# Queries and index queries of a sparse-attention block: features on the partitions, stacked per head by way of DRAM in place of PE transposes

## The chip, the cores and the metric

The kernel runs on one core of one Trainium2 chip. Its five engines run side by side, each with its own instruction stream in order: TensorE (PE, matmuls; its weight loads are shown as PEld), VectorE (DVE), ScalarE (ACT), GpSimd (POOL) and SyncE (SP, which here only issues DMAs). They wait for each other by semaphores. Sixteen DMA engines move data between DRAM and the on-chip memory; SP, ACT and POOL each issue to a queue of their own. PE writes its results to eight banks of accumulator memory, and ACT or DVE carry them from there.

The metric is the device time of one execution in microseconds (us), as the median over runs. Before the change it is 763.98 us (three runs, 763.91 to 766.41).

## The reference, cut to what matters

Two layers run over 528 tokens (16 meta tokens ahead of 512) of 1024 features. Every layer projects the normed input into queries (8 heads of 64), one key and one value head, index queries (8 heads of 64), one index key, gates and pooling inputs. Each layer chooses, for every query, the 128 keys with the best index score among those it may see, and attends to these.

```python
q, k, v, gate_a, u_b, gate_b, q_idx, k_idx, w_idx, merge = jnp.split(proj, ...)
q = apply_rope(rms_norm(q.reshape(B, T, N_HEADS_A, HEAD_DIM), qn_g), cos_h, sin_h)
k = apply_rope(rms_norm(k, kn_g), cos, sin)
q_idx = apply_rope(q_idx.reshape(B, T, N_IDX_HEADS, IDX_DIM), cos_h, sin_h)
k_idx = apply_rope(k_idx, cos, sin)
attn = indexer_sparse_attention(q, k, v, q_idx, k_idx, w_idx, k_top)
...
def apply_rope(x, cos, sin):
    half = x.shape[-1] // 2
    rot = jnp.concatenate([-x[..., half:], x[..., :half]], axis=-1)
    return x * cos + rot * sin
```

`apply_rope` is where the two halves of a head, features 0 to 31 and 32 to 63, are mixed: the first half becomes a cos - b sin, the second b cos + a sin.

## The kernel before

**Numbers in two parts.** Products that need more precision than one pass gives are made from a high part (a value rounded to the fast fp32r format) and a low part (what the rounding left). The normed input lies in `hhi` and `hlo`, with features on the partitions and tokens in the free dimension; every weight chunk has a high tile and a low tile. A product is three sums: high by high, low by high, high by low. With 8 blocks of 128 input features that makes 24 matmuls, called a group here.

**Weights.** They come in chunks of 256 output columns (`chunks`, lines 112 to 128), two chunks ahead of their use, by SP into the tiles `raw` (`w_fetch`). `w_prep_enqueue` queues the splitting into high and low: as ACT cast and DVE subtraction (`high`, `low`), or, for chunks in `by_dma`, as a negated ACT copy, an accumulating DMA from POOL's queue (line 202) and a second ACT copy. In each layer chunk 0 and chunk 2 hold the index queries of heads 0 to 3 and 4 to 7, chunk 1 the keys, values and index weights (used unsplit), 3 and 4 and 8 and 9 gates, 5 and 6 the pooling inputs, 7 and 10 the attention queries of heads 0 to 3 and 4 to 7.

**Order.** PE's and DVE's instructions run in the order in which the program writes them; a scheduler orders the other engines and the DMA queues by readiness. Each product group ends with `group_done`, which counts groups, runs what `later(fn, n)` has put n groups off, takes one step of weight splitting, and calls `half_done`. That one, also called in the middle of a group, takes `rate` / 2 steps on average from the queue `fill`, whose entries are generators: `index_steps` (the index scores, lines 627 to 640) and later the attention. Steps of the top-k search (`sel`) are taken when an estimate says that DVE has time. So PE meets the first index step of a tile at a fixed place in its own stream and waits there if the tile isn't complete. `drain` empties `fill` before the pooling inputs.

**A query tile.** `tok_group` (line 481) makes a [128 tokens x 256 features] tile, four heads, with the tokens as stationary operand: 24 matmuls with 256 columns moving. `q_post` (line 585) takes it on: two DVE products with cos and sin tables (the second with the halves swapped) and their sum on POOL; for attention queries also a square on ACT and a sum per head on DVE for the norm (`RQ`, applied later as a scale in the softmax). Groups later follow `second` (ACT casts the high part), `third` (DVE subtracts the low part) and `trans`: four PE transposes, one per head, of [128 tokens x (64 high, 64 low)], and an ACT copy of their bank. The result for each head is a [128 x 128] operand with 64 rows of high parts above 64 of low parts and tokens in the free dimension: `qi` for the index scores, `qq` for the attention, the stationary operands of products with the stacked keys `KI` and `KK`.

**Stages of a layer** (lines 1041 to 1169). A trio of key groups; then index groups for token tiles 1 and 2, key groups for tiles 3 and 4, index groups for tiles 3 and 4 (chunk 0), four index groups from chunk 2; the gate products of chunks 3 and 4; the pooling inputs; `queries(0)` (chunk 7), gates, `queries(1)` (chunk 10); then the attention as fill beside the branch products. In layer 0 `queries` has a fifth tile, the 16 meta tokens, whose normed queries go to `qm`. `index_steps` of a tile enters `fill` FI = 6 groups after its own group; `rate` is 3 in this stage (`R_IDX`) and until the attention. `tables` lets POOL build cos and sin tables times the norm gains, four times in all.

**Tiles.** Temporary tiles share places by tag: six of tag L (544 columns; `r` of the index steps and the attention's rows among them), four of tag P (the stacked parts ahead of their transposes), six of tag tt, eight of tag B (`qi`, `qq` and others).

Of the kernel before, what the change touches and what calls it, by code (L numbers as in the profile page):

```python
# [17 lines left out]
T = 528  # L18
# [11 lines left out]
PB = 4  # L30
R_ATT = (1.95, 1.7)
# [9 lines left out]
R_IDX = 3  # L41
UF = 2
QI = 3
# [45 lines left out]
def tile_block(ctx: ExitStack, tc: tile.TileContext, x, meta, w_in, pool_w, w_a, w_b, w_out, rows, hgain, c_tab, out):  # L89
# [10 lines left out]
    def f(ap):  # L100
        return ap.bitcast(F32)
# [11 lines left out]
    mixed, by_dma, plain = set(), set(), set()  # L113
    for l in range(2):
        wi = w_rows(w_in[l], 0, w_in.shape[2])

        chunks.append([(wi[:, :, 2176:2432], 0)])
# [6 lines left out]
        by_dma |= set(range(len(chunks) - 10, len(chunks)))  # L124
# [38 lines left out]
    def w_prep_enqueue(casts_first=False, after=None):  # L163
# [14 lines left out]
        def split(which):  # L178
            t = w_tile().rearrange("p (k e) -> p k e", e=cols)
            parts[which].extend(t[:, k] for k in range(kt // 2))  # L180
            return t

        his = {}

        def high(s):
            his[s] = split(0)
            act.copy(his[s], raws[c][s])

        def low(s):
            dve.tensor_sub(split(1), raws[c][s], f(his[s]))  # L190
# [193 lines left out]
    gains = one.tile([128, 2, 2, 64], F32, name="gains")  # L384
# [7 lines left out]
    dma(gains, bass.AP(tensor=hgain.tensor, offset=hgain.offset, ap=[[0, 128], [128, 2], [64, 2], [1, 64]]))  # L392
# [27 lines left out]
    Cg = one.tile([128, 5, 64], F32, name="Cg")  # L420
    Sg = one.tile([128, 5, 64], F32, name="Sg")
    BV = one.tile([128, 4, 2, 64], F32, name="BV")
    RQ = one.tile([128, 4, NH], F32, name="RQ")
    NR = one.tile([128, 4, NH], F32, name="NR")
# [4 lines left out]
    def sheet(n, name):  # L429
        if n > HB:  # L430
            return tmp.tile([128, 544], F32, tag="L", name=name, bufs=LB)
        return tmp.tile([128, HB], F32, tag="tt", name=name, bufs=6)

    def tables(l, keys):
        if keys:
            gk = tmp.tile([128, 64], F32, tag="gk", name="gk", bufs=1)
            gp.tensor_scalar(gk, gains[:, 1, l], -0.125, None, op0=OP.mult)
        g = gk if keys else gains[:, 0, l]

        def bc(g):  # L440
            return g[:, None, :].to_broadcast([128, 5, 64])

        def sw(g):
            return g.rearrange("p (a d) -> p a d", a=2)[:, None, ::-1, :].to_broadcast([128, 5, 2, 32])

        s4 = stab.rearrange("p t (a d) -> p t a d", a=2)
        gp.tensor_tensor(Cg, ctab, bc(g), op=OP.mult)
        gp.tensor_tensor(Sg.rearrange("p t (a d) -> p t a d", a=2), s4, sw(g), op=OP.mult)
# [32 lines left out]
    def tok_group(t, w):  # L481
        e = 256
        s, m = TOK[t]
        ps = bank("d")
        for h in H:
            for k in range(KT):
# [883 lines left out]
```

## Time and profile before

| | |
|---|---|
| median of three runs | 763.98 us |
| the profiled execution | 764.77 us |
| its span on the core | 763.0 us |
| instructions in the span | 15629 |
| bytes moved by DMA | 96.94 MB, 127 GB/s |

The page of the profile and its views are of that one execution. A line of the timeline has the start, the duration, the engine, the line in the program (nearly all PE and DVE instructions carry the line of a helper, L61), the operation, the written tile, the tiles that were read, shapes and count. For a matmul "128*16" is the size of the stationary operand and "128x256" the moving one. Durations of neighbouring matmuls overlap, so costs on PE are taken from starts, not from durations. A plain fp32 matmul leaves two records. In the list of groups the last numbers are the busy time in all, the mean in ns, and the engine's idle time ahead of the group with what ended it. In a view of windows each row has the window, its length, then busy time and count of instructions for PE, PEld, DVE, ACT and POOL, the granted clock, the share of the DMA engines and GB/s. A DMA's row has its size and the median time from issue to landing. In the page's line of DMA shares each digit is a fortieth of the span, in tenths.

### The profile page before, as it was taken

Reading aid. Unit: us, or ns where it says so; the run is one execution under the profiler, and the core shown is the slowest. Engines: PE = TensorE matmul, PEld = TensorE weight load, DVE = VectorE, ACT = ScalarE, POOL = GpSimd, SP = SyncE. Lnnn points to the kernel's source line nnn. Section 1 sums busy time; section 2 is a strip of 40 time slices with the busy share of each in tenths; the row PEclk is TensorE's granted clock in tenths of the full one; section 3 lists DMA queues with packets and bytes.
Section 4 is the critical chain, followed back from the end, with each engine's and each line's share of the span. In section 5 each row is a group of like instructions: output and inputs, shape, how many; then the busy total and the mean of one; then the engine's idle time right before and its main releaser. Section 6 shows DMA issues by size and latency. Waiting matters only on the chain.

```text
span 763.0 us, 15629 instructions
## 1 busy us (share of the span) xinstructions
PE 746.0 (98%) x5911; PEld 712.7 (93%) x5911; DVE 555.8 (73%) x1412; ACT 471.4 (62%) x1044; POOL 214.2 (28%) x282
## 2 busy tenths in 40 slices
PE   6999999999999999999999999999999999999998
PEld 5899999999999999999998989988889899999998
DVE  4866887888888776894447668877899888678531
ACT  5668844638788796543245796455577788864320
POOL 2551174334011010063346410761411111005200
PEclk9999999999999999999999999999999999999999
DMA  7567685676031112553422677678811221146411
GB/s 257 179 157 194 151 198 138 142 195 165 2 107 60 56 58 82 168 170 112 140 85 83 166 172 169 172 152 204 204 49 56 85 83 56 57 123 213 138 44 42
DMA packets 73547, 96.94 MB, mean 127 GB/s; under 512 B 3664, under 2 KB 58736, under 8 KB 73472
## 3 DMA queue, kind: packets, MB, share of 16 engines
q1 hardware_dynamic: 67488, 74.83, 30.8%
q0 software_dynamic: 5760, 20.97, 15.1%
q8 instruction: 46, 0.75, 0.4%
q14 instruction: 29, 0.24, 0.1%
q10 hardware_dynamic: 224, 0.15, 0.1%
HBM read 66.41 MB, written 8.55 MB: 98 GB/s over the span
## 4 chain that ended last, share of the span: by engine, by line
PE 79%; DVE 11%; ACT 7%; issue 1%; DMA 1%; POOL 0%; ACTq 0%; DVEq 0%; POOLq 0%
PE d L61 66%; PE a L61 10%; PE v L61 4%; DVE w L61 3%; ACT lt L713 2%; ACT w L233 1%; ACT lt L724 1%; DVE t L61 1%; DVE raw L61 1%; DVE nf L61 1%; DMA par<-in_rows_dram 1%; ACT pt L740 1%; DVE lt L61 1%; DVE c L61 1%; DVE alo L61 1%
## 5 line engine op out<-in xcount | busy, mean ns | idle before, releaser
L61 PE MATMUL d<-hhi,w 128*128 128x256 f32 (+3 forms) x1408 | 287.8, 296 | 0.3 <-DVE c L61 0.2
L61 PEld LDWEIGHTS d<-hhi,w 128*128 128x128 f32 x1408 | 225.9, 188 | 6.1 <-DVE c L61 0.7
L61 PE MATMUL d<-hlo,w 128*128 128x256 f32 (+3 forms) x704 | 193.6, 294 | 0.6 <-DVE hlo L61 0.6
L61 PEld LDWEIGHTS d<-hlo,w 128*128 128x128 f32 x704 | 132.5, 188 | 3.3 <-DVE hlo L61 0.8
L61 PE MATMUL d<-w,hhi 128*128 128x256 f32 (+1 forms) x800 | 124.9, 286 | 0.7 <-DVE w L61 0.5
L61 PEld LDWEIGHTS d<-w,hhi 128*128 128x128 f32 (+1 forms) x800 | 107.3, 185 | 3.8 <-issue 1.2
L61 DVE TENSOR_TENSOR w<-raw,w 128x512 fp32r<-128x512 f32 (+1 forms) x128 | 107.8, 852 | 2.4 <-ACT w L233 2.3
L61 PE MATMUL d<-hsum,w 128*128 128x264 f32 (+1 forms) x576 | 77.1, 286 | 0.1
L725 POOL TENSOR_SCALAR pm<-lt,rs 128x16 f32<-128x16 f32 x48 | 27.3, 583 | 173.5 <-DVE rs L61 166.6
L61 PE MATMUL d<-w,hlo 128*128 128x256 f32 (+1 forms) x400 | 74.5, 281 | 0.0
L61 PEld LDWEIGHTS d<-hsum,w 128*128 128x128 f32 x576 | 71.8, 188 | 1.1 <-ACT lt L724 0.3
L202 POOL DMA_DIRECT2D w<-raw x40 | 36.8, 935 | 104.7 <-ACT w L201 82.7
L233 ACT CAST w<-raw 128x512 fp32r<-128x512 f32 x96 | 56.8, 623 | 3.6 <-DVE raw L61 3.5
L61 PEld LDWEIGHTS d<-w,hlo 128*128 128x128 f32 (+1 forms) x400 | 58.5, 184 | 0.4
L1233 POOL TENSOR_TENSOR hlo<-ta,hhi 128x256 fp32r<-128x256 f32 (+1 forms) x28 | 28.2, 1021 | 96.6 <-PE d L61 84.1
L61 DVE MATCH_REPLACE8 sc<-m,sc 128x400 f32<-128x400 f32 (+2 forms) x100 | 54.3, 548 | 0.0
L61 DVE MAX8 m<-sc 128x8 f32<-128x400 f32 (+2 forms) x100 | 52.7, 556 | 0.8
L713 ACT ACTIVATE lt<-lt,mn,NR 128x144 f32<-128x144 f32 (+3 forms) x64 | 42.3, 665 | 16.5 <-DVE mn L61 16.3
L61 PE MATMUL d<-mhi,w 128*128 128x272 f32 (+2 forms) x192 | 47.6, 328 | 0.0
L201 ACT ACTIVATE w<-raw 128x1024 fp32r<-128x1024 f32 x40 | 41.3, 1057 | 10.2 <-PE d L61 10.2
L61 DVE SCALAR_TENSOR_TENSOR sc<-r,wsg,sc 128x144 f32<-128x144 f32 (+3 forms) x56 | 32.4, 581 | 16.6 <-ACT r L637 14.1
L602 POOL TENSOR_TENSOR t<-t,t 128x256 f32<-128x256 f32 (+1 forms) x34 | 31.1, 916 | 39.4 <-DVE t L61 39.4
(198 smaller groups left out, 1392.1 us busy)
## 6 DMA issues: line engine op xcount, KB each, us to landing
raw<-in_w_in_dram SPq DMA_DIRECT2D x72, 512.0 KB, 3.6
w<-raw POOLq DMA_DIRECT2D x40, 512.0 KB, 5.7
raw<-in_w_out_dram SPq DMA_DIRECT2D x16, 512.0 KB, 3.4
kept<-res SPq DMA_DIRECT2D x16, 264.0 KB, 2.8
res<-kept SPq DMA_DIRECT2D x16, 264.0 KB, 6.1
raw<-in_w_branch_b_dram SPq DMA_DIRECT2D x8, 512.0 KB, 4.2
raw<-in_w_branch_a_dram SPq DMA_DIRECT2D x8, 512.0 KB, 3.7
xt<-in_x_dram SPq DMA_DIRECT2D x4, 512.0 KB, 6.3
```

The costliest lines, as they stand in the source:

```text
L61: return fn(*a, **k)
L201: act.activation(t, raws[c][s], AF.Copy, scale=-1.0)
L202: gp.dma_start(t, raws[c][s], accum_op=OP.add)
L233: act.copy(t[:, 0], blk[src[n]])
L602: gp.tensor_tensor(t1[:m, :256], t1[:m, :256], t2[:m, :256], op=OP.add)
L713: act.activation(L[hh][:, :n], L[hh][:, :n], AF.Exp, scale=NR[:, i, h:h + 1], bias=mn[:, hh:hh + 1], accum_out=sm[:, hh:hh + 1])
L724: act.activation(L[hh][:, 16:n], L[hh][:, 16:n], AF.Copy, scale=rs[:, hh:hh + 1])
L725: (gp if j < 3 else dve).tensor_scalar(pms[i][:, 2 * j + hh, :], L[hh][:, 0:16], rs[:, hh:hh + 1], None, op0=OP.mult)
L740: act.copy(pt[:, :2 * len(bs)], tp[:, :256 * len(bs)].rearrange("p (a c) -> p a c", c=128))
L1233: pool_end = gp.tensor_sub(hlo[:, j, a:a + n], d, f(hhi[:, j, a:a + n]))
```

## The change

A query pair replaces two query tiles. `query_pair` makes, for half of the tokens, four heads at once: two groups (`dense` with `turn`) with the weights as stationary operand and the tokens moving. The weight chunks 0, 2, 7 and 10 are `turned`: split with their columns reordered, so that the first group gives the first rotary halves of the four heads (4 x 32 features on the partitions) and the second group the second halves. All four are split by ACT and DVE; 7 and 10 no longer by accumulating DMA. `first` multiplies a group by cos and sin (`CS`, both tables turned once at the start by 20 matmuls) and, for attention queries, by the gain per feature (`gq`) in one DVE instruction with two output halves; POOL combines the halves of both groups. `second` casts the high part, `third` subtracts the low part and writes both, head by head, into a DRAM tile `via` whose rows are in the stacked order (eight DMAs from SP); `fourth` reads the stacked tiles back (two DMAs from POOL, three with the meta tokens). There are no transposes of queries any more. The norms' sums of squares over features become two small PE products per pair (`norms`). Meta tokens ride in the first half of layer 0's queries; their scale is applied in `meta_attn`. Index steps enter `fill` five groups after the pair's own two; `rate` becomes 4 (`R_GATE`) behind the index stage. `tables` is gone; `kv_post` multiplies by the key gain itself. Tag tt has five places instead of six.

```diff
+        turned |= {len(chunks) + i for i in (0, 2, 7, 10)}
...
-        by_dma |= set(range(len(chunks) - 10, len(chunks)))
+        by_dma |= set(range(len(chunks) - 10, len(chunks))) - turned
...
+            if c in turned:
+                parts[which].extend(t.rearrange("p (a k e) -> p k a e", a=2, k=4)[:, k] for k in range(4))
+                return t.rearrange("p (a h d) -> p a h d", a=2, d=32)
...
+            return raws[c][s].rearrange("p k (h a d) -> p a (k h) d", a=2, d=32) if c in turned else raws[c][s]
...
+    for h in range(4):
+        dma(gq[32 * h:32 * h + 32].rearrange("p l a -> p (l a)"),
+            bass.AP(tensor=hgain.tensor, offset=hgain.offset, ap=[[1, 32], [32, 4]]))
...
+    def turned_tables():
...
+        for c, tab in enumerate((ctab, stab)):
+            for ts_ in ((0, 1, 2), (3, 4)):
+                tp = bank("a")
...
+                    for o in (0, 64):
+                        pe.matmul(tp[o:o + 64, s - a:s - a + m], tab[:m, t], ident[:m, :m], start=True, stop=True)
...
-    def tok_group(t, w):
...
-    def q_post(t, ps, normed, dst, g=0):
...
+    def query_pair(l, g, hf, w, normed, dst, between=None):
+        a, n = (HB, T - HB) if hf else (0, HB) if normed and l == 0 else (16, HB - 16)
+        M, sq = [None, None], [None, None]
+        via = dram.tile([128, 4, n], F32, name=f"via{l}{g}{hf}{int(normed)}")
+        rows_of = via.rearrange("(s a d) h t -> s h d a t", s=2, a=2)
+
+        def first(b, ps):
+            m = M[b] = tmp.tile([128, 544], F32, tag="L", name="turned", bufs=LB)[:, :2 * n].rearrange(
+                "p (c n) -> p c n", c=2)
+            p2 = ps[:, None, :n].to_broadcast([128, 2, n])
+            if normed:
+                dve.scalar_tensor_tensor(m, p2, gq[:, l, b:b + 1], CS[:, :, a:a + n], op0=OP.mult, op1=OP.mult)
+                sq[b] = tmp.tile([128, HB], F32, tag="tt", name="sq", bufs=TB)[:, :n]
+                act.activation(sq[b], ps[:, :n], AF.Square, scale=HD ** -0.5)
+            else:
+                dve.tensor_tensor(m, p2, CS[:, :, a:a + n], op=OP.mult)
+            if b:
+                gp.tensor_tensor(M[0][:, 0], M[0][:, 0], m[:, 1], op=OP.subtract)
+                gp.tensor_tensor(M[0][:, 1], M[0][:, 1], m[:, 0], op=OP.add)
...
+        def second():
+            t = part("qhi")[:, :2 * n].rearrange("p (c n) -> p c n", c=2)
+            parts.append(t)
+            act.copy(t, M[0])
+            if normed:
+                dve.tensor_add(sq[0], sq[0], sq[1])
+
+        def third():
+            t = part("qlo")[:, :2 * n].rearrange("p (c n) -> p c n", c=2)
+            dve.tensor_sub(t, M[0], f(parts[0]))
+            parts.append(t)
+            for s, p in enumerate(parts):
+                for h in range(4):
+                    dma(rows_of[s, h], f(p[32 * h:32 * h + 32]))
+            if normed:
+                norms()
+
+        def norms():
+            sp = bank("a")
+            for x_ in range(2):
+                o = TOK[1 + 2 * hf + x_][0] - a
+                pe.matmul(sp[:, 4 * x_:4 * x_ + 4], sq[0][:, o:o + 128], heads4, start=True, stop=True)
...
+        def fourth():
+            todo = [(dst[x_], TOK[1 + 2 * hf + x_][0] - a, 128) for x_ in range(2)]
+            if a == 0:
+                todo.append((qm[:, 4 * g:4 * g + 4], 0, 16))
+            for d, o, m in todo:
+                gp.dma_start(d, via[:, :, o:o + m])
+
+        for b in range(2):
+            ps = dense(w, b, a, n, turn=True)
+            later(lambda b=b, ps=ps: first(b, ps), 1)
+            if b:
+                for k, fn in enumerate((second, third, fourth)):
+                    later(fn, 2 + k)
+            if between:
+                between(b)
+            group_done()
...
+        def index_queries(hf, g, w, between=None):
+            qi = [tmp.tile([128, 4, 128], F32R, tag="B", name="qi", bufs=8) for _ in range(2)]
+            query_pair(l, g, hf, w, False, qi, between)
+            for x_ in range(2):
+                later(lambda x_=x_: fill.append(index_steps(2 * hf + x_, g, qi[x_])), FI - 1)
...
+        index_queries(0, 0, w, second_half)
+        for t in (3, 4):
+            ps = plain_group(t, raws[kv])
+            later(lambda t=t, ps=ps: kv_post(l, t, ps), 1)
             group_done()
...
+        index_queries(1, 0, w)
...
+        for hf in range(2):
+            index_queries(hf, 1, w, lambda b, hf=hf: keep(2 * hf + b))
...
+        rate[0] = R_GATE
```

More of the change, by code (lines that the diff above doesn't have):

```diff
@@ L30 @@
 PB = 4
+TB = 5
 R_ATT = (1.95, 1.7)
@@ L41 @@
 R_IDX = 3
+R_GATE = 4
 UF = 2
-QI = 3
 LEAD = 5
```

216 lines of the change are left out of this document (90 added, 126 removed).

## The prediction

> **What bounds the kernel now.** I read the engines' busy shares first, then the chain of work that ended last, then what the TensorE (PE) waited for.
>
> ```profile
> PE 746.0 (98%) x5911; PEld 712.7 (93%) x5911; DVE 555.8 (73%) x1412; ACT 471.4 (62%) x1044; POOL 214.2 (28%) x282
> ...
> DMA  7567685676031112553422677678811221146411
> ...
> PE 79%; DVE 11%; ACT 7%; issue 1%; DMA 1%; POOL 0%; ACTq 0%; DVEq 0%; POOLq 0%
> ```
>
> PE is busy for 746.0 of 763.0 us, and 79% of the chain is its work. Of PE's own waits the edit touches one, of transposes for their operand:
>
> ```profile
> PE a L61 <- DVE qs L61: 0.4, 1, 0.4
> ```
>
> So the change is worth the PE work that it removes, less what it adds, less the waits that it puts in PE's in-order stream. I call the two token (or feature) groups of an index pair A1, A2 (first half of the tokens, heads 0 to 3), A3, A4 (second half), B1 to B4 (heads 4 to 7), the late key groups K3, K4, and the gate groups behind them C1 to C8. PE runs A1 A2 K3 K4 A3 A4 B1..B4 C1..C8.
>
> **PE work removed.** One index group with the transposes around it, and an output group without any, from the chain of waits:
>
> ```profile
> 56.69 0.45 PE L61 MATMUL a<-identr,qs 128*128 128x128 f32 x4
> 56.98 1.18 PE L61 MATMUL d<-w,hhi 128*128 128x256 f32 x8
> ...
> 59.89 0.46 PE L61 MATMUL a<-identr,qs 128*128 128x128 f32 x4
> ```
> ```profile
> 60.79 1.51 PE d L61 x12
> ...
> 65.27 1.43 PE d L61 x12
> ...
> 710.93 2.84 PE d L61 x24
> ```
>
> From transposes to transposes it is 59.89 - 56.69 = 3.20 us, against 2.84 us for 24 bare matmuls: 0.36 us for four transposes and the restart. There are 128 of them:
>
> ```profile
> L61 PE MATMUL a<-identr,qs 128*128 128x128 f32 x128 | 14.7, 238 | 0.4 <-DVE qs L61 0.4
> ...
> L61 PE MATMUL d<-w,hhi 128*16 128x256 f32 x32 | 4.6, 285 | 0.0
> ```
>
> 128 / 4 x 0.36 = **11.5 us**. The new groups have 24 matmuls of 256 columns as the old ones do, only with weights as the stationary operand, so they cost the same 2.84 us. The 16 meta tokens, though, had a group of their own in each query chunk of layer 0 (the second row above counts 32 of its 48 matmuls), at the full 256 columns:
>
> ```profile
> 119.87 1.10 PE L61 MATMUL d<-w,hlo 128*16 128x256 f32 x8
> 120.80 1.10 PE L61 MATMUL d<-w,hhi 128*16 128x256 f32 x8
> 121.75 1.05 PE L61 MATMUL a<-us,pw 128*128 128x272 f32 x4
> ...
> 132.13 0.48 PE L61 MATMUL a<-identr,qs 16*128 16x16 f32 x4
> 132.54 1.21 PE L61 MATMUL d<-w,hhi 128*128 128x256 f32 x8
> ```
>
> Sixteen take 121.75 - 119.87 = 1.88 us, so 24 take 2.82, and the small transposes 0.41: twice 3.2 = **6.5 us**. In exchange 96 matmuls have 272 columns, which is 1.51 against 1.43 us per 12 in the chain above, so +0.6 us.
>
> **PE work added.** The squares are now summed over partitions by matmuls with one full fp32 tile as weights. The row statistics of the output stage are that form:
>
> ```profile
> 398.36 0.28 PE L61 MATMUL a<-ones,sqs 128*128 128x1 f32 x2
> ...
> 399.24 2.88 PE L61 MATMUL v<-raw,nf 128*16 128x200 f32 x16
> ```
>
> Four such matmuls lie between 398.36 and 399.24 (two records each), 0.22 us each; 18 of them (two in each of 8 query pairs, two for the meta tokens) and eight restarts of 0.07 are 4.5 us. The turned cos and sin tables need 20 half-array fp32 matmuls of 128 columns, once. The attention's value products are that form:
>
> ```profile
> 205.30 2.11 PE v L61 x24
> ...
> 230.76 2.99 PE v L61 x40
> ```
>
> Both have the same four meta products; the 16 further records (8 matmuls) cost 0.88 us, 0.11 each, so 2.2 us. PE work in all: -11.5 - 6.5 + 0.6 + 4.5 + 2.2 = **-10.7 us**.
>
> **The new trip through DRAM.** Per pair SP issues eight 64 KB writes, four for the high part and four for the low part; POOL then issues two 256 KB reads (three with the meta tokens) that wait for all eight. No such trip is in the trace; these are its nearest rows:
>
> ```profile
> raw<-in_w_in_dram SPq DMA_DIRECT2D x72, 512.0 KB, 3.6
> ...
> kept<-res SPq DMA_DIRECT2D x16, 264.0 KB, 2.8
> ...
> out_dram<-ot SPq DMA_DIRECT2D x16, 128.0 KB, 1.7
> far<-nf SPq DMA_DIRECT2D x4, 264.0 KB, 4.6
> ...
> hsheet<-far SPq DMA_DIRECT2D x3, 264.0 KB, 3.7
> ```
> ```profile
> L202 POOL DMA_DIRECT2D w<-raw x40: 850/876/1288, 49.0 to 546.4; - x40
> ...
> DMA to landing us min/median/max: 4.5/5.7/8.5
> ```
> ```profile
> L1316 SPq DMA_DIRECT2D out_dram<-ot x16: 332/332/356, 714.5 to 760.2; - x16
> ```
>
> Four issues at 0.33 us, after the last low part, are 1.4 us. A write lands between 1.7 us (quiet) and 4.6 us (busy stage); I take 2.8, the row with the same burst of writes to DRAM. The read lands between 3.7 and 8.5 us; I take 5.0, half the bytes of the POOL row but 512 short runs. The trip is 1.4 + 2.8 + 5.0 = 9.2 us behind the low part; bounds 6.8 and 14.5.
>
> When is the low part there? Its place in VectorE's order (DVE) is that of the old one, `third`:
>
> ```profile
> 38.43 0.42 DVE L61 TENSOR_TENSOR qs<-t,qs 128x256 fp32r<-128x256 f32 x1
> ...
> 51.20 0.42 DVE L61 TENSOR_TENSOR qs<-t,qs 128x256 fp32r<-128x256 f32 x1
> ```
> ```profile
> 34.55 2.95 PE L61 MATMUL d<-raw,nf 128*128 128x200 f32 x16 [0.63 <-DVE t L61]
> 37.43 1.27 PE L61 MATMUL a<-identr,ks 16*128 16x16 f32 x12
> 38.54 1.18 PE L61 MATMUL d<-w,hhi 128*128 128x256 f32 x8
> ...
> 52.99 0.46 PE L61 MATMUL a<-identr,ks 128*128 128x128 f32 x4
> ```
>
> For the first tile it ran 1.0 us after K4's end at 37.43; for the third, due behind B2, 1.8 us before B2's end at 52.99. The new one is twice as wide (0.7 us), so it ends 1.7 us after its group in pair A1-A2 and 1.1 us before it in the others. PE asks for the result three groups on, when the first index step comes out of the fill queue. Pair A1-A2: twelve key transposes (38.54 - 37.43 = 1.1), three groups (8.5), four key transposes (0.36): 10.0 us, against 1.7 + 9.2 = 10.9, so PE waits **0.9 us in each layer**. Pair A3-A4: B3, B4, C1 and some five index steps, about 10.5 us, against 8.1, no wait. For B1-B2 and B3-B4 the gates and up to eight steps make it 13 and 11.5 us, no wait. The attention queries are asked for later still: the third unit of the attention, first to read heads 4 to 7, is seven fill steps behind the last pair at 1.95 a group.
>
> The Trainium skill's page "DMA: Bandwidth & Descriptors" (Anatomy of one DMA) puts a transfer at 2.0 us plus its bytes at 436 GB/s, about 2.2 us for a write and 2.6 for a read here as an estimate; by that no pair waits and the sum would be 1.8 us lower. Its section Rules for kernel authors speaks against the change (under 64 KB a transfer is mostly overhead), and the row of 4.6 us for 264 KB shows that this fit is a quiet chip's.
>
> **Everything else.** Chunks 7 and 10 of each layer are now split by ACT and DVE instead of an accumulating DMA: 8 more wide DVE subtractions, 8 fewer ACT passes.
>
> ```profile
> L61 DVE TENSOR_TENSOR w<-raw,w 128x1024 fp32r<-128x1024 f32 x32 | 42.9, 1357 | 0.1
> ...
> L201 ACT ACTIVATE w<-raw 128x1024 fp32r<-128x1024 f32 x40 | 41.3, 1057 | 10.2 <-PE d L61 10.2
> ...
> L61 DVE TENSOR_TENSOR qs<-t,qs 128x256 fp32r<-128x256 f32 x32 | 13.3, 416 | 0.0
> ```
>
> That is +10.9 us on DVE and -8.5 on ACT. Against it two old tiles cost DVE six 256-wide operations (2.5 us; the attention queries also two reductions and two small adds), a new pair three 512-wide ones at about 0.7 (the attention queries also one add). Over 16 pairs that is about -9 us, so DVE keeps its load, and ACT loses its 32 evictions. While top-k still runs there is little room: PE 19.9 and DVE 19.0 of 20 us here.
>
> ```profile
> 560.00:580.00 20.00, 19.92 (x131) 17.29 (x130) 19.02 (x57) 14.61 (x41) 1.34 (x5) 1.00 0.06 17
> ```
>
> I charge 1.0 us (bounds 0 and the refund below). At B1, PE already waits for DVE's low halves of chunk 2; when it comes 0.7 us sooner it waits that much more, but that is the same place as the 0.9 us above, so the two overlap. The four tiny gain loads at the start hold SP back by four issues, 1.3 to 1.6 us; the second half of the kv weights behind them is not read before the middle of the first key group, so nothing is charged (at worst 1.5). The rotary tables that POOL no longer builds were off PE's path.
>
> **Sum.** 764.77 (profiled run, 763.0 span and 1.8 around it) - 10.7 + 2 x 0.9 + 1.0 = 756.9; that run lies 0.8 above the median of 763.98, so **756.1 us**.
>
> **Rivals.** (1) *Loaded queues, slower than before.* One mechanism: write and read together take 4.6 + 8.5 = 13.1 us instead of 7.8, because the stage's DMA queues are full (the page's DMA line has 5 to 8 tenths in the first ten slices). With x us more, a layer's waits are 0.9 + x, then x - 2.4, x - 3.4 and x - 4.9 where positive. At x = 5.3 that is 6.2 + 2.9 + 1.9 + 0.4 = 11.4, twice 22.8: 764.77 - 10.7 + 22.8 + 1.0 - 0.8 = 777. It ends above the old time once a layer loses 4.9 us, at x = 3.2. For it: POOL's 512 runs of 512 bytes have no row. Against: raw loads of 1 KB runs land in 3.6 us in the same stage. (2) *The refund.* PE's saving behind the index stage (16 tiles at 0.36, the 6.5, less 5.1) is 7.2 us; if DVE sets the pace of top-k and softmax, all of it comes back as a burst before the attention: 763.3, no change. For it: the last row above; against: PE lost only 0.1 us in that window. (3) *Buffers.* The products take places of the six L tiles that the index steps rotate through (about 2.2 beside the steps' 3.5); should the steps wait for a place, 1.5 us in each of eight index pairs gives 768. PE's four small banks cover most of that.
>
> **Chances.** Forecast 0.56, refund 0.14, loaded queues 0.24, buffers 0.06. No change means within 0.5%, about what a measurement of this kernel can tell: 760.2 to 767.8. Faster 0.57, no change 0.18, slower 0.25. The forecast's own range is 752 (no wait, nothing lost on DVE, and 1 us for the terms) to 760; the range of 8 in 10 reaches to 772, where x is 4.6.
>
> **What would show it.** Right: the rows of transposes with qs and of the 128*16 groups are gone, each index pair's first KI product follows its group with under 1 us idle, and the read lands in about 5 us. Wrong: PE idle in front of KI products at B1 and C1 released by the DMA that fills qi (rival 1), by ACT's r (rival 3), or DVE full from the queries to the attention with PE idle there (rival 2).

## The result, and the profile after

| | time, us (median) | against the kernel before |
|---|---|---|
| before | 764.3 (763.9 to 766.4, 4 runs) | 1 |
| after | 775.1 (772.3 to 777.2, 4 runs) | 1.0133, interval 1.0105 to 1.0162 |

The change makes the kernel 1.3% slower; 756.1 was predicted. The profiled execution of the changed kernel took 772.29 us, 770.5 of it the span. The same parts of the page as before:

```profile
span 770.5 us, 15586 instructions
PE 738.5 (96%) x5803; PEld 705.3 (92%) x5803; DVE 564.8 (73%) x1341; ACT 448.6 (58%) x996; POOL 223.2 (29%) x292
PEclk9989999999999999999999899999999999999999
DMA  7588966879332112543422899568981221136411
PE 69%; DMA 9%; DVE 9%; ACT 7%; issue 3%; SPq 1%; POOL 1%; ACTq 0%; DVEq 0%; POOLq 0%
```

PE's busy time fell by 7.5 us and the span rose by 7.5. DMA, 1% of the chain before, is 9% now, and PE's granted clock, full in all slices before, is no longer full in two, one near the start of each layer. Two landmarks in each layer say where: ScalarE's copies of the pooling input (u), behind the index stage, and of the gate product (zb), behind the attention queries. Both come from the view of a tile: count, duration in ns, and the start of the first and of the last. Before:

```profile
L1138 ACT COPY u<-d x8: 364/379/439, 97.1 to 119.2; 128x272 f32<-128x272 f32 x4, 128x256 f32<-128x256 f32 x4
L1196 ACT COPY zb<-d x16: 348/368/392, 177.8 to 204.7; 128x272 f32<-128x272 f32 x8, 128x256 f32<-128x256 f32 x8
L1138 ACT COPY u<-d x8: 362/380/388, 474.0 to 496.1; 128x272 f32<-128x272 f32 x4, 128x256 f32<-128x256 f32 x4
L1196 ACT COPY zb<-d x8: 563/569/593, 550.1 to 572.6; 128x512 f32<-128x512 f32 x8
```

After:

```profile
L1193 ACT COPY u<-d x8: 362/380/390, 104.5 to 126.6; 128x272 f32<-128x272 f32 x4, 128x256 f32<-128x256 f32 x4
L1251 ACT COPY zb<-d x16: 350/368/390, 178.9 to 206.8; 128x272 f32<-128x272 f32 x8, 128x256 f32<-128x256 f32 x8
L1193 ACT COPY u<-d x8: 363/379/387, 483.6 to 505.7; 128x272 f32<-128x272 f32 x4, 128x256 f32<-128x256 f32 x4
L1251 ACT COPY zb<-d x8: 560/578/586, 558.2 to 579.7; 128x512 f32<-128x512 f32 x8
```

From the last u to the first zb, the stage with the attention queries, it is 52.3 us instead of 58.6 in layer 0 and 52.5 instead of 54.0 in layer 1: 7.8 us won, where the prediction's terms for this stage make 7.2 (16 x 0.36 and 6.5, less 4.5 for the norms and 0.6 for the 272 columns, which only these queries have). But the first u comes 7.4 us later in layer 0, and 9.6 later in layer 1. Of these 9.6, 1.1 were there at layer 0's first zb and 3.4 when layer 0's attention was through (the last copy of the branches' own u starts at 314.1 before and at 317.5 after). So the two index stages lose 7.4 and about 6 us, and layer 0's attention 2.3. Two of PE's own waits (us in all, times, the longest) come first here; then the first index pair of layer 0 goes through its trip, in order of time (start, duration, engine; in brackets the idle time before, and what ended it):

```profile
PE a L62 <- DMA qi<-via: 13.9, 6, 5.4
PE d L62 <- DVE w L62: 1.9, 2, 0.9
```
```profile
38.62 0.72 DVE L62 TENSOR_TENSOR qlo<-turned,qhi 128x512 fp32r<-128x512 f32 x1 [1.09 <-ACT sq L546]
39.62 1.80 SPq L637 DMA_DIRECT2D via<-qlo  x4
...
45.86 1.64 POOL L614 TENSOR_TENSOR turned<-turned 128x256 f32<-128x256 f32 x1 [5.17 <-DVE turned L62]
47.47 1.71 POOL L615 TENSOR_TENSOR turned<-turned 128x256 f32<-128x256 f32 x1
49.12 1.76 POOL L666 DMA_DIRECT2D qi<-via  x2
...
49.22 0.45 PE L62 MATMUL a<-identr,ks 128*128 128x128 f32 x4
54.95 0.67 PE L62 MATMUL a<-KI,qi 128*128 128x144 f32 x2 [5.28 <-DMA qi<-via]
```

The low part is ready at 39.34 and PE gets the tiles at 54.95: 15.6 us, where the prediction had 9.2. The middle rows were not in the prediction. POOL stands from 40.7 to 45.86 at the sums (L614) of the **next** pair, whose product VectorE hasn't made yet; the two sums then run for 1.64 and 1.71 us, and only then POOL issues the read of the first pair, which stands behind them in its queue. Layer 1 repeats it: sums at 425.26, read at 428.52, a wait of 5.40 us that ends at 434.47.

While PE waits, its clock goes. Stretches around that wait (length, busy time of PE, PEld, DVE, ACT and POOL with instructions, granted clock, DMA share, GB/s):

```profile
46.00:52.00 6.00, 2.71 (x20) 2.16 (x19) 3.87 (x4) 2.80 (x5) 5.79 (x5) 1.00 0.63 174
52.00:54.00 2.00, 0.00 (x0) 0.00 (x0) 0.00 (x0) 1.20 (x2) 0.89 (x2) 0.50 1.48 311
...
56.00:58.80 2.80, 2.80 (x15) 2.80 (x15) 0.29 (x1) 1.13 (x3) 0.00 (x0) 0.50 1.06 222
58.80:62.00 3.20, 3.20 (x30) 3.20 (x30) 1.71 (x4) 1.53 (x5) 0.76 (x2) 1.00 0.49 110
```

The clock is half from 52 to 58.8, and PE does 15 matmuls in 2.80 us there against 30 in 3.20 behind it. The Trainium skill's page "TensorE: Matmul & The Clock Gate" (What's actually happening) has this half clock after an idle window of about 3.4 us; here it came at most 2.4 us after PE's last product, and PE had stood 0.9 us once before, until 48.64.

### The profile page after: what moved, and what is told of

Same layout as the page of the kernel before. It is cut to its first block, busy times and chain, and to the rows that moved or that the text cites. A ratio compares the mean times of both kernels' runs of the same rounds, so it can differ in the third digit from the quotient of the medians.

```text
span 770.5 us, 15586 instructions
## 1 busy us (share of the span) xinstructions
PE 738.5 (96%) x5803; PEld 705.3 (92%) x5803; DVE 564.8 (73%) x1341; ACT 448.6 (58%) x996; POOL 223.2 (29%) x292
## 4 chain that ended last, share of the span: by engine, by line
PE 69%; DMA 9%; DVE 9%; ACT 7%; issue 3%; SPq 1%; POOL 1%; ACTq 0%; DVEq 0%; POOLq 0%
PE d L62 58%; PE a L62 8%; PE v L62 3%; DMA via<-qhi 3%; DMA qi<-via 2%; ACT lt L766 2%; DMA via<-qlo 2%; DVE w L62 2%; SPq L637 1%; ACT w L243 1%; ACT lt L777 1%; DVE raw L62 1%; DMA far<-nf 1%; DVE lt L62 1%; ACT pt L793 1%
## 5 line engine op out<-in xcount | busy, mean ns | idle before, releaser
L62 PE MATMUL d<-hhi,w 128*128 128x256 f32 (+3 forms) x1920 | 386.4, 294 | 2.1 <-DVE w L62 1.9
L62 PEld LDWEIGHTS d<-hhi,w 128*128 128x128 f32 x1920 | 307.5, 189 | 10.1 <-DVE w L62 2.7
L62 PE MATMUL d<-hlo,w 128*128 128x256 f32 (+3 forms) x960 | 257.9, 292 | 0.1
L62 PEld LDWEIGHTS d<-hlo,w 128*128 128x128 f32 x960 | 182.3, 190 | 3.8 <-issue 1.0
L62 DVE MAX8 m<-sc 128x8 f32<-128x400 f32 (+2 forms) x100 | 52.6, 555 | 0.9
L197 ACT CAST w<-raw 128x1024 fp32r<-128x1024 f32 x40 | 41.9, 1049 | 12.1 <-PE d L62 8.5
L62 PE MATMUL d<-w,hhi 128*128 128x256 f32 x256 | 47.7, 287 | 0.0
L690 ACT ACTIVATE r<-a,wab 128x272 f32<-128x272 f32 (+2 forms) x80 | 34.3, 487 | 18.8 <-PE a L62 18.8
L62 PE MATMUL a<-KI,qi 128*128 128x272 f32 (+3 forms) x160 | 28.2, 305 | 13.9 <-DMA qi<-via 13.9
L62 PEld LDWEIGHTS d<-w,hhi 128*128 128x128 f32 x256 | 39.2, 189 | 0.0
L62 PEld LDWEIGHTS a<-KI,qi 128*128 128x128 f32 x160 | 24.3, 197 | 16.2 <-issue 6.5
```

The lines of the kernel that those rows point to most:

```text
L62: return fn(*a, **k)
L197: act.copy(his[s], raw_of(s))
L690: act.activation(r[:, n - 1::-1] if i == 0 else r[:, o:o + e], ps[:, :e], AF.Relu, scale=wab[:, i, h:h + 1])
```

## The experiments

Three theories stood at the start. **Theory 1:** the order in POOL's queue makes the read late. **Theory 2:** the trip is too slow in itself, beside the stage's other transfers. **Theory 3:** what PE is spared comes back through VectorE or ScalarE, whatever the waits do. All results, each as a ratio to the kernel before, run beside it:

| run | us | ratio to before (95%) |
|---|---|---|
| order | 771.7 | 1.0093 (1.0075 to 1.0111) |
| dve_sums | 769.6 | 1.0058 (1.0041 to 1.0075) |
| two_later | 770.9 | 1.0095 (1.0069 to 1.0122) |
| index_by_pe | 760.8 | 0.9952 (0.9937 to 0.9967) |
| no_wait | 762.3 | 0.9966 (0.9955 to 0.9977) |
| kept_busy | 778.6 | 1.0189 (1.0155 to 1.0224) |
| two_writes | 768.9 | 1.0058 (1.0035 to 1.0082) |
| dve_sums_two_later | 772.6 | 1.0097 (1.0065 to 1.0130) |
| dve_sums_no_wait | 758.4 | 0.9911 (0.9889 to 0.9933) |
| half_trip | 770.6 | 1.0072 (1.0049 to 1.0095) |
| half_trip_128 | 762.2 | 0.9969 (0.9950 to 0.9987) |
| queries_by_dram_first | 781.8 | 1.0225 (1.0201 to 1.0249) |
| two_writes_pool | 764.2 | 0.9998 (0.9986 to 1.0011) |
| two_writes_act | 766.7 | 1.0022 (1.0001 to 1.0043) |

### Which half of the change loses: index_by_pe

```diff
-    turned |= {len(chunks) + i for i in (0, 2, 7, 10)}
+    turned |= {len(chunks) + i for i in (7, 10)}
...
-            query_pair(l, g, hf, w, False, qi, between)
+            ps = tok_group(t, w)
+            later(lambda: q_post(t, ps, qi), 1)
```

> The index queries go back to token groups and PE transposes as before the change, the other queries stay as changed. Theories 1 and 2 (the loss is the index pairs' late reads): the A to U stages are as before, the query stages keep what they had gained (6.2 us in layer 0, 1.4 in layer 1, 1.4 at the start partly), so 755 to 760. Theory 3 (what PE is spared comes back elsewhere): 763 to 770.

760.8 us, just above the 755 to 760 of Theories 1 and 2, and 3.5 faster than before: the attention queries through DRAM are a gain, and the index queries through DRAM cost 775.1 - 760.8 = 14.3 us. Theory 3 as a refund of everything is out, but a part of it shows. In layer 0 it is 139.0 us from the first zb to the branches' last u, 136.3 before, and PE stands for 4.3 of the 140 us from 180 to 320, 1.9 before. Its waits for ScalarE's softmax are longer there, and the last top-k maximum starts at 200.3 instead of 194.4; what holds these up wasn't followed.

### POOL's queue: order and dve_sums

```diff
-                gp.tensor_tensor(M[0][:, 0], M[0][:, 0], m[:, 1], op=OP.subtract)
-                gp.tensor_tensor(M[0][:, 1], M[0][:, 1], m[:, 0], op=OP.add)
+                with tc.issue_after(last_read[0]) if last_read[0] is not None else nullcontext():
+                    gp.tensor_tensor(M[0][:, 0], M[0][:, 0], m[:, 1], op=OP.subtract)
+                    gp.tensor_tensor(M[0][:, 1], M[0][:, 1], m[:, 0], op=OP.add)
...
-                gp.dma_start(d, via[:, :, o:o + m])
+                last_read[0] = gp.dma_start(d, via[:, :, o:o + m]).ins
```

> The two POOL sums of a query pair are queued behind the read that was issued last; of the index pairs only the second of each layer changes place (its sums stood ahead of the first pair's read). Theory 1 (the order in POOL's queue makes the read late): the first pair's read is issued about 3.3 us earlier in each layer, the wait of PE in front of the key products falls from 5.3 to about 2 us, the granted clock stays up there, and the time falls by 6 to 10 us, to 765 to 769. Theory 2 (the trip through DRAM is itself too slow beside the other transfers): the read lands when it did, the waits stay at 5.3 us and the time at 775. Theory 3 (the time comes back through VectorE, whatever the waits do): the waits shrink and the time stays above 772.

771.7: 3.4 us off the changed kernel where Theory 1 had 6 to 10. The read of the first pair now goes at 45.41, and PE's wait for it is gone; but others have come in its place, and in all PE still waits 9.2 us for reads (13.9 in the changed kernel). Here are POOL and PE in layer 0, then VectorE and SP at the second pair:

```profile
45.41 1.76 POOL L669 DMA_DIRECT2D qi<-via  x2 [3.24 <-DMA via<-qlo]
...
63.55 1.57 POOL L669 DMA_DIRECT2D qi<-via  x2 [5.71 <-DMA via<-qhi]
...
67.77 1.64 PE L62 MATMUL a<-KI,qi 128*128 128x400 f32 x4 [2.79 <-DMA qi<-via]
...
52.38 0.69 DVE L62 TENSOR_TENSOR qlo<-turned,qhi 128x512 fp32r<-128x512 f32 x1 [0.80 <-ACT qhi L630]
52.37 4.18 SPq L640 DMA_DIRECT2D via<-qhi  x4
56.65 3.82 SPq L640 DMA_DIRECT2D via<-qlo  x4
```

The second pair's low part is ready at 53.07, and SP needs until 60.47 to issue eight writes (0.33 us each in the prediction), the read goes at 63.55 and PE has the tiles at 67.77: 14.7 us without any sums in the way. Theories 1 and 2 both hold, each for a part.

```diff
-                gp.tensor_tensor(M[0][:, 0], M[0][:, 0], m[:, 1], op=OP.subtract)
-                gp.tensor_tensor(M[0][:, 1], M[0][:, 1], m[:, 0], op=OP.add)
+                eng = gp if normed else dve
+                eng.tensor_tensor(M[0][:, 0], M[0][:, 0], m[:, 1], op=OP.subtract)
+                eng.tensor_tensor(M[0][:, 1], M[0][:, 1], m[:, 0], op=OP.add)
```

> The two sums of the index pairs run on VectorE instead of POOL (16 of them in the program, about 0.42 us each by the row of the other two-input subtraction of that size), so that nothing but weight moves stands ahead of a read in POOL's queue. Theory 1: as the run with the changed order, and the second pair's read comes earlier too; the sums themselves no longer take 1.6 and 1.7 us beside VectorE; 763 to 768. Theory 2: 775. Theory 3 (VectorE is the bound there): slower than after, 777 to 780.

769.6, above the 763 to 768 of Theory 1, but the better of the two though VectorE has more to do. PE still waits 8.1 us for reads, at the second and third pair of layer 0 and the second of layer 1.

### How much is the wait: no_wait and dve_sums_no_wait

```diff
-                later(lambda x_=x_: fill.append(index_steps(2 * hf + x_, g, qi[x_])), FI - 1)
+                later(lambda x_=x_: fill.append(index_steps(2 * hf + x_, g, hhi[:, 0:4, TOK[1 + 2 * hf + x_][0]:TOK[1 + 2 * hf + x_][0] + 128])), FI - 1)
```

> All work and all transfers of the changed kernel stay, but the index products multiply the normed tokens instead of the index queries, so that nothing waits for the tiles that come back from DRAM; what is left out is the use of the index queries, so the keys that are picked are others. If the loss is PE's wait for these reads and what follows from it (theories 1 and 2, with the clock): the DMA waits go, the clock stays up, and the time is that of the run with the index queries by PE less its 64 transposes of 0.074 us, 755 to 758. If the time comes back through VectorE or ScalarE (theory 3): 763 or more.

762.3, between the two. With every transfer in place and nobody waiting for the tiles, 12.8 us of the loss are gone, but not all. What is left shows in POOL's and ScalarE's order in layer 0:

```profile
63.94 1.57 POOL L666 DMA_DIRECT2D qi<-via  x2 [5.16 <-DMA via<-qlo]
...
66.66 1.45 POOL L614 TENSOR_TENSOR turned<-turned 128x256 f32<-128x256 f32 x1
...
68.83 0.62 ACT L627 CAST qhi<-turned 128x512 fp32r<-128x512 f32 x1 [4.10 <-POOL turned L615]
```

A read that waits in POOL's queue for its writes holds back the sums of a later pair, these hold back ScalarE's copy, and behind the copy stand the evictions that free PE's banks: PE waits up to 1.4 us for them. It is the same queue as before, the other way round. The next run takes the sums out of it as well.

> The sums of the index pairs on VectorE, and the index products multiply the normed tokens instead of the index queries (their use is left out, all transfers stay). In the run without the wait alone, ScalarE still stood 4.1 us behind sums that stood in POOL's queue behind a read, and PE 1.7 us behind ScalarE, in each layer. If POOL's queue (a read that waits there for its data) is the second part of the loss: these go and the time is 757 to 759. If ScalarE or the transfers are simply too full: 761 to 763 as without this change.

758.4, inside the 757 to 759 that POOL's queue was to give. So the changed kernel's distance to one in which nobody waits for the tiles and the sums are out of POOL's queue is 775.1 - 758.4 = 16.7 us: POOL's sums account for 762.3 - 758.4 = 3.9 with the wait away and for 775.1 - 769.6 = 5.5 with it, the wait for the tiles itself for 769.6 - 758.4 = 11.2.

### Why the trip is slow: two_writes, half_trip, and two other queues

```diff
+        if not normed:
+            via = dram.tile([2, 128, 2, n], F32, name=f"via{l}{g}{hf}")
+            heads_of = via.rearrange("s (h d) a t -> s a d h t", h=4)
...
+                if not normed:
+                    dma(via[s], f(p))
...
+                    for e in range(4):
+                        gp.dma_start(d[32 * e:32 * e + 32], heads_of[e // 2, e % 2, :, :, o:o + m])
```

> On top of the run with the sums on VectorE: the index pairs' tiles are written as they lie, one transfer each for the high and the low part instead of four, and the rearrangement is made by the reads, four of 32 partitions for each block instead of one; bytes and the count of 512 byte pieces that are read stay. If the writes are late because eight transfers for each pair wait in SP's queue (4 to 8 us for the eight there): they land within 5 us of the low part, PE's waits fall from 8 to 3 us or less and the time to 765 to 768. If the transfers themselves are slow: the waits stay or grow with POOL's 6 us of issues for each pair, 769 to 773.

768.9, no different from the sums on VectorE alone (769.6), and PE waits as long for reads, 8.6 us. The number of SP's issues was not the limit: the second pair's low part is now a single write, issued at once, and still not there for ten microseconds. (POOL's reads take more issues now; that isn't separated here.)

```profile
48.62 1.52 SPq L145 DMA_DIRECT2D raw<-in_w_in_dram  x2
51.88 0.34 SPq L641 DMA_DIRECT2D via<-qlo  x1
...
62.24 2.68 POOL L677 DMA_DIRECT2D qi<-via  x5 [9.30 <-DMA via<-qlo]
...
69.31 1.67 PE L62 MATMUL a<-KI,qi 128*128 128x400 f32 x4 [4.66 <-DMA qi<-via]
```

The next run, again with the sums on VectorE, takes away load: half the bytes and half the writes.

```diff
+                if s and not normed:
+                    continue
                 for h in range(4):
                     dma(rows_of[s, h], f(p[32 * h:32 * h + 32]))
...
-                gp.dma_start(d, via[:, :, o:o + m])
+                e = 128 if normed else 64
+                gp.dma_start(d[:e], via[:e, :, o:o + m])
...
-                pe.matmul(ps[:, :w], qS[:, hh, :], KI[0][:, 0, o:o + w], start=True, stop=False)
-                pe.matmul(ps[:, :w], qS[:, hh, :], KI[0][:, 1, o:o + w], start=False, stop=True)
+                pe.matmul(ps[:, :w], qS[:64, hh, :], KI[0][:64, 0, o:o + w], start=True, stop=False)
+                pe.matmul(ps[:, :w], qS[:64, hh, :], KI[0][:64, 1, o:o + w], start=False, stop=True)
```

> On top of the sums on VectorE: only the high parts of the index queries go through DRAM, four writes and half the read for each pair, and the index products leave the low parts out (64 rows instead of 128; PE's time for a product goes by its columns). If the count of transfers and bytes on queues that were already loaded makes the reads late: PE's waits for them fall from 8 to 3 us or less, the clock stays up and the time is 760 to 764. If the trip's fixed parts make it late: the waits stay above 6 us and the time at 767 to 770.

No wait for the index queries' reads is left in PE's waits, as expected of loaded queues, but the time was 770.6, no better than 769.6. The cut had a price of its own, for PE's time did not go by columns alone: products of 64 rows between products of 128 were dearer here. In layer 0 the 80 index products take 13.9 us, each counted to PE's next start, against 10.6 in dve_sums_no_wait, and the matmuls around them are slower too. So it was repeated with 128 rows, the lower half zeros:

```diff
+            for q in qi:
+                gp.tensor_copy(q[64:128], none[64:128, :, None].to_broadcast([64, 4, 128]))
```

> As the run with half the trip, but the index products keep their 128 rows: rows 64 to 127 of the tiles are zeros that POOL writes ahead of time, so that the low parts are left out and PE's products are those of the changed kernel. In the run with 64 rows the waits for the reads were gone and PE's index products took 13.9 us instead of 10.6 in layer 0. If the count of transfers and bytes on loaded queues is what makes the reads late: no wait over 1 us for them here either, and the time is that of the run with the sums on VectorE and no wait, 757 to 761. If the reads were only in time there because PE was slower: the waits come back, 3 us or more in total, and 763 to 769.

762.2 (759.4 to 767.1 in 7 runs), between the two expectations: the profiled execution, the slowest of them, still has two waits for reads, 4.4 us in all. Half the trip's load gives back 7.4 of the 11.2 us, but not at layer 0's second pair, for which PE waits 2.8 us (1.4 in dve_sums). The last three of that pair's four writes still land 10.8 to 11.5 us after their issue. Beside them SP has issued two weight loads and POOL two accumulating transfers, 512 KB each, between 50.9 and 52.6. What the trip's load is added to shows in the stretches of the kernel before:

```profile
48.00:56.00 8.00, 7.76 (x67) 7.56 (x67) 4.99 (x14) 6.91 (x15) 3.48 (x4) 1.00 1.03 248
52.00:64.00 12.00, 12.00 (x102) 12.00 (x101) 6.14 (x15) 9.10 (x18) 4.41 (x6) 1.00 0.85 199
64.00:76.00 12.00, 12.00 (x104) 12.00 (x103) 9.18 (x17) 10.26 (x23) 0.00 (x0) 1.00 0.76 190
76.00:88.00 12.00, 12.00 (x97) 12.00 (x97) 8.77 (x24) 8.64 (x18) 1.74 (x2) 1.00 0.83 197
```

and of the changed one:

```profile
64.00:76.00 12.00, 12.00 (x97) 12.00 (x97) 7.54 (x15) 8.88 (x16) 5.05 (x7) 1.00 1.04 212
76.00:88.00 12.00, 11.28 (x93) 11.09 (x92) 8.42 (x17) 10.29 (x22) 3.29 (x4) 1.00 1.28 305
```

In windows of 12 us the DMA engines were busy for 0.76 to 0.85 of this stage before the change. But the mean hides that in the 8 us from 48 on, where the second pair's trip now falls, their share was 1.03 already, with weight transfers alone. With the change the share stays above 1 later too, that is, the packets' times overlap. Whether SP's queue, with its weight loads, is a bottleneck of its own was still open. Two runs issue the same two writes elsewhere:

```diff
-                    dma(via[s], f(p))
+                    gp.dma_start(via[s], f(p))
```

> As the run with two writes, but the two writes are issued by POOL instead of SP. In that run one write of the low part, alone and issued at once at 51.88, still landed only at about 62; SP's queue had taken two weight loads of 512 KB from 48.62 on, just ahead of it. If the writes are late because they stand behind weight loads in SP's queue: they land within 5 us here, PE's waits for the reads fall under 3 us in total and the time to 759 to 764. If all queues share the same full engines: the waits stay at 6 to 9 us and the time at 767 to 772.

The second has act.dma_start there.

> As the run with two writes, but issued by ScalarE, each behind the instruction that it waits for; ScalarE stands still until VectorE has the low part, about 1 us for each pair. If SP's queue is the cause: writes land within 5 us, PE's waits fall under 3 us and 760 to 765. If the engines are full: 767 or more.

764.2 and 766.7, so 4.7 and 2.2 us off two_writes (the second is not clear of the spread of the runs), and PE's waits for the reads are 3.8 and 3.9 us instead of 8.6. Both times lie between the two expectations: SP's queue has a part. But the second pair's low part takes as long as ever from either queue. POOL's run and ScalarE's run (the read waits for that write in both):

```profile
53.10 0.58 POOL L641 DMA_DIRECT2D via<-qlo  x1 [0.93 <-DVE sc L62]
...
63.40 2.82 POOL L677 DMA_DIRECT2D qi<-via  x5 [8.06 <-DMA via<-qlo]
```
```profile
52.02 0.33 ACTq L641 DMA_DIRECT2D via<-qlo  x1
...
61.94 4.31 POOL L677 DMA_DIRECT2D qi<-via  x8 [8.34 <-DMA via<-qlo]
```

From SP, POOL and ScalarE the read behind that 256 KB write can go 10.4, 10.3 and 9.9 us after the write's issue: that points to the transfer engines, which all three share (their busy share from 52 to 64 us was 1.04 in two_writes and 1.08 in two_writes_pool), rather than to a queue. In each of the three runs the weight load that SP had issued 2.1 to 2.4 us ahead of that write took 11.2 to 11.5 us as well. How engines and queue divide the loss over the other pairs stays open.

### More time for the trip: two_later and dve_sums_two_later

```diff
-                later(lambda x_=x_: fill.append(index_steps(2 * hf + x_, g, qi[x_])), FI - 1)
+                later(lambda x_=x_: fill.append(index_steps(2 * hf + x_, g, qi[x_])), FI + 1)
```

> The index steps of a pair enter the fill two groups later, about 5 us of PE work; order and transfers are as in the changed kernel. Theories 1 and 2 both: PE's 5.3 us waits in front of the key products nearly go and the clock stays up, 761 to 766, as long as later index steps cost nothing. Theory 3 (refund): the steps are pushed together in the gates and in front of the pooling, PE waits for ACT or VectorE there instead, 770 or more.

> Both changes in one: the sums of the index pairs on VectorE and the index steps two groups later. If what two groups cost is only the place of the steps (theory 3 for the top-k rounds, which start later): no waits for DMA are left and the time stays at 767 to 771. If waits alone decide: 758 to 762.

770.9 and 772.6, so neither comes near the times of waits that simply go (761 to 766, and 758 to 762). No wait for a read is left among PE's longest waits, but ScalarE is waited for in two places instead. Waits of two_later:

```profile
PE a L62 <- ACT lt L777: 5.2, 5, 2.0
PE a L62 <- ACT r L690: 3.4, 3, 2.1
```

The first is the softmax (1.2 us of waits in the changed kernel). VectorE's top-k rounds start about when they did but end far later, and the attention, which begins 4 us earlier here (ScalarE's first softmax step is at 178.1 instead of 182.3), runs into them. Their maxima in layer 0, with the first and the last start, in the changed kernel:

```profile
L62 DVE MAX8 m<-sc x50: 292/568/695, 91.0 to 205.8; 128x8 f32<-128x272 f32 x16, 128x8 f32<-128x400 f32 x16, 128x8 f32<-128x528 f32 x16, 128x8 f32<-128x144 f32 x2
```

and in two_later:

```profile
L62 DVE MAX8 m<-sc x50: 293/568/696, 91.8 to 223.3; 128x8 f32<-128x272 f32 x16, 128x8 f32<-128x400 f32 x16, 128x8 f32<-128x528 f32 x16, 128x8 f32<-128x144 f32 x2
```

The last is 17.5 us later (24.6 in layer 1). The second wait is the index steps' evictions, which now come while ScalarE stands for other things; in dve_sums_two_later, layer 1, for a weight load that takes ten microseconds beside the trip's writes:

```profile
440.33 1.09 SPq L145 DMA_DIRECT2D raw<-in_w_in_dram  x2
...
451.54 1.06 ACT L211 ACTIVATE w<-raw 128x1024 fp32r<-128x1024 f32 x1 [8.04 <-DMA raw<-in_w_in_dram]
```

So here Theory 3's picture is right, more than in index_by_pe: the time made for the trip is taken from the top-k rounds and the softmax behind them.

### What the half clock costs: kept_busy

```diff
+            def keep_busy():
+                ps = bank("d")
+                for _ in range(22):
+                    nc.tensor.matmul(ps[:, :512], hhi[:, 0, 16:144], hhi[:, 0, 16:528], start=True, stop=True)
+                yield from ()
+            if (hf, g) == (0, 0):
+                later(lambda: fill.append(keep_busy()), FI - 1)
```

> In the changed kernel, 22 products of 512 columns (5.1 us at the full clock) whose result nobody reads stand on PE in front of the first index products of each layer, where it stood idle for 5.3 us. If the half clock behind such a wait costs time of its own: no half clock in either place, and 771 to 772, about 3.8 us less than the changed kernel, although PE has 10 us more to do. If the clock is a mark of the wait and costs nothing beside it: 775; if the read comes later because of it: more.

778.6, more than the changed kernel (the two intervals overlap a little), the last of the three. The clock does stay full at both places, but in layer 0 PE meets a wait of 3.3 us at a later pair's read instead (0.7 there in the changed kernel), and in layer 1 one of 2.1 (1.3). In all, PE's waits for these reads fall by 8.5 us, to 5.4, and its busy time grows by 10.6. The half clock is real, and PE is slower while it lasts, but that it lengthens the run was not shown.

### A try for a better version: queries_by_dram_first

```diff
-        order = [2432, 1664, 1920, 1408, 1152, 0, 640, 896, 256]
+        order = [2432, 1664, 1920, 1408, 1152, 0, 256, 640, 896]
...
         queries(0)
+        queries(1)
...
-        queries(1)
```

> The run with the index queries by PE, and the second group of queries directly behind the first, ahead of the attention gate, so that its read has the gate's 18 to 20 us of PE work to land in. What is to go: PE's waits of 1.9 us (layer 0) and 1.6 us (layer 1) at the start of the attention. 757 to 760 if nothing else moves; 761 or more if the top-k rounds, which run on VectorE then, are pushed back by the queries' products.

781.8, far off. The weights that come next are late now, and so are ScalarE's evictions behind them:

```profile
PE a L63 <- ACT lt L822: 5.3, 4, 4.0
PE d L63 <- ACT zb L1293: 3.9, 1, 3.9
PE d L63 <- DMA w<-raw: 3.8, 2, 2.5
```

Which of the three starts it wasn't followed up. The best version found is index_by_pe, 760.8 us.

## Why the prediction was wrong

- **PE's work: nearly right.** The sum was -10.7 us; in dve_sums_no_wait PE is busy for 736.5 us instead of 746.0, 9.5 less. The query stages gave 7.8 of 7.2. For the index pairs, index_by_pe against dve_sums_no_wait is 2.4 us, where 64 transposes at 0.36 per four were 5.8: by PE's starts in the trace of before, a transpose is 0.074 us, so 64 are 4.8, and some of that goes into the wait for chunk 2 named below. The turned tables' 20 matmuls took 2.5 us from start to start, where 2.2 was charged.
- **The step that failed: the trip's 9.2 us and the 0.9 us of wait that came of it.** I summed issue, write and read (1.4 + 2.8 + 5.0) and let POOL issue the read as soon as the writes have landed. The first pair's trip took 15.6 us, and PE waited 5.3 us for it (5.4 in layer 1). For the first pair the pieces I had were nearly right: in the run with the changed order issue and write took 4.6 us from the low part (40.80 to 45.41) against 4.2, and the read in the changed kernel 5.8 against 5.0. What was missing is POOL's queue: the next pair's sums stand ahead of the read, and the read went at 49.12 where it could have gone at about 44. The prediction doesn't ask in which order POOL has the sums and the read.
- **For the second pair onward the size was wrong.** No wait was predicted for A3-A4, with 10.5 us to spare against 8.1 behind B2; the trip there takes 14.7 us as soon as the first pair isn't holding everything up. Rival 1 had the mechanism of this part, loaded queues, and with its own price came to 777 against 775 measured. That it came so near is partly luck: it has 22.8 us of waits for the reads where the trace has 13.9, and knows nothing of POOL's order. I gave it 0.24. Against it I held one landing time, 3.6 us for the weight loads "in the same stage"; but that is the median over the whole execution, and in the stage itself (46 to 66 us) five weight loads and four of POOL's accumulating transfers took 3.4 to 8.5 us. The row that bears on it is the DMA share before the change, 1.03 from 48 to 56 us, and I read only the page's line for it, in tenths, as evidence for the rival and not as a bound on the trip.
- **The wait for chunk 2's low halves** was predicted to grow and to overlap with the wait for the trip. It grew to 0.9 us a layer and didn't overlap: PE waits for the weights at 47.7 and for the tiles at 49.7.
- **VectorE's 1.0 us and the refund: seen in part.** With the waits away the time is 758.4, but that it lies close to the 756.1 forecast is partly luck, for without its 1.8 us of waits the forecast is 754.3. PE does 1.2 us more work there than forecast, and it stands idle 3.2 us longer than before (20.2 instead of 17.0) where 1.0 was charged. Some of that is in layer 0's attention, where index_by_pe and the changed kernel lose 2.7 and 2.3 us too. The refund grows when the index steps are moved back.
- **Buffers (rival 3): not the cause.** ScalarE's r is waited for, but because ScalarE stands behind POOL's sums: with the sums on VectorE and no wait it is 0.7 us.
- **The half clock** wasn't foreseen; it shows in the trace, and a cost to the run as a whole wasn't shown.

## What to carry to other kernels

Before a step is moved to DMA, read the DMA engines' share in that very stage, in windows as short as the trip: here 0.76 to 0.85 over 12 us hid 8 us at 1.03, and a write there took 10 us to land from any of three queues, while the price came from landing times elsewhere. Then write out the order of each queue that the trip uses: a transfer that waits for data at the head of an engine's queue stops that engine's arithmetic, and arithmetic that waits there stops the transfer. The same trip was a gain for the attention queries, whose result was asked for later.

## What the runs showed of the hardware that I had not expected

- PE's clock was half at most 2.4 us after its last product in layer 0 (1.8 in layer 1), and for 6.8 us, so into the work behind the wait.
- POOL's sums of 128x256 took 1.64 and 1.71 us in the rows above, while VectorE subtracted weight tiles, and half that a little later:

```profile
45.70 2.88 DVE L62 TENSOR_TENSOR w<-raw,w 128x1024 fp32r<-128x1024 f32 x2
...
61.24 0.74 POOL L614 TENSOR_TENSOR turned<-turned 128x256 f32<-128x256 f32 x1 [8.34 <-DVE turned L62]
```

  The Trainium skill's page "SBUF — State Buffer" (Who interferes with whom) has a VectorE instruction with two SBUF inputs contend with a GpSimd instruction that reads SBUF; the rows agree.
- Index products of 64 rows among products of 128 cost PE 13.9 us in layer 0 and 14.0 in layer 1; for the same columns with 128 rows half_trip_128 has 11.3 in layer 0 and 10.6 in layer 1.
